# A two-block model on one core: where the small columns' pool stands in memory, and 256 bytes in front of the last phase's tiles

## The chip, the core and the metric

The kernel runs on one core of a Trainium2 chip. The metric is the device time of one launch in microseconds (us), the median of the runs. TensorE (PE in the rows) does the matrix products, VectorE (DVE), ScalarE (ACT) and GpSimd (POOL) do the rest, SyncE (SP) issues most of the transfers. TensorE's weight loads have rows of their own, PEld.

## The reference

An activation of 512 tokens by 1024 features goes through two blocks of two layers each.

```python
h = h + even_mixer(rmsnorm(h))      # x @ w_in, 31-tap convolution, pooling, gates, @ w_out
h = h + odd_mixer(rmsnorm(h))       # x @ w_in, 4-tap convolution, gated recurrence, @ w_out
x = rmsnorm(h)
# second block, layer 0: state-space mixer; layer 1: windowed attention
for i in range(2):
    h = h + mix_i(rmsnorm(h))
    h = h + square(relu(rmsnorm(h) @ w_up[i])) @ w_down[i]      # 1024 -> 4096 -> 1024
    h = h + sigmoid(rmsnorm(h) @ w_gate[i]) * (p[i] @ w_proj[i])
return rmsnorm(h)
```

## The kernel before

The activation stands feature-major: eight tiles `h[k]` of 128 features by 512 tokens. A product with a weight matrix goes output tile by output tile. `get_w` hands out one chunk of 128 by 1024 weights; `prep` has loaded it (SP's queue, tile `raw`), and split it into a high and a low part, `hi` by ScalarE (L225) and `lo` by VectorE or GpSimd (L228). The moving operand is split in the same way. `mm3` then makes three matmuls for each 128 by 128 block of weights, lines L284 to L286:

```python
        mm(out, hi[:, sl], xh, start=start, stop=False)
        mm(out, hi[:, sl], xl, start=False, stop=False)
        mm(out, lo[:, sl], xh, start=False, stop=stop)
```

Each has its own weight load of 128 columns, which runs beside the matmul ahead of it, and moves 512 columns of 4 bytes a partition, 2048 bytes. A block of weights is 512 bytes a partition, so all blocks of a chunk start at the same place modulo 512.

Memory is given out as a stack of pools, in the order of their making; a pool's size is the sum of its tags' buffers. The ones that stay are made in `__init__`: `const`, `raw` (2 tiles of 4096 bytes a partition), `whi` and `wlo` (3 of 4096 each: the tiles `hi` and `lo`), `h` (10 of 2048), `xg` (16 of 2048: split moving operands) and `small` (columns: four buffers each of `v`, `rs`, `st` and `sm`; `v` has 16 bytes and is kept in 32, the others have 64, 96 and 96; 1152 bytes in all). Above them `phase` opens one pool of SBUF tiles (`l`) and one of PSUM banks for each part of the run, and closes them at its end; tiles made by `L` and `LR` stand there. From the first MLP on, a pool `m` lies below the phase's pool (tiles of 2048 bytes: `acc`, two `sq`, `rs`).

Moving operands, by the pool in which they stand:

- `xg`: inputs of the mixers, of both MLPs (`w_up`), of keys and values.
- the phase's pool: `big` (even mixer), `d`, `xs` and `y` (odd mixer's output product, and the gated unit behind the state-space mixer), `o` (queries, half of attention's output), `hid` (second product of both MLPs, `w_down`, and the gate's product in `ple`).

A few weights stand in the phase's pool too: `wrh` and `wrl` of the odd mixer, and the first chunks of the gated unit, which `prep` puts into tiles named `x` and `gt`, since the regular ones are not free yet.

The order of instructions on each engine comes from the framework's scheduler. The pool of a phase is opened with waits tile by tile: a tile waits for the tiles of earlier phases that stood where it stands.

In the last phase `mlp` makes two halves of 16 `w_up` tiles (`xg` moving, tile `r`, then `hid`) and 8 `w_down` tiles (two chunks each), and `ple` makes 8 gate tiles of 24 matmuls (`hid` moving; the last one in halves of 256 columns). `ple` fetches the tiles `pj` on GpSimd's queue (L1333).

Of the kernel before, what the change touches and what calls it, by code (L numbers as in the profile page):

```python
# [7 lines left out]
F32 = mybir.dt.float32  # L8
# [29 lines left out]
class Vecs:  # L38
    def __init__(self):
        self.parts, self.at, self.n = [], {}, 0  # L40
# [116 lines left out]
class Kern:  # L157
# [10 lines left out]
    def __init__(self, ctx, tc, I, O, vat, cat):  # L168
        self.tc, self.nc, self.I, self.O = tc, tc.nc, I, O
        self.vat, self.cat = vat, cat  # L170
        P = lambda name, bufs, **k: ctx.enter_context(tc.tile_pool(name=name, bufs=bufs, **k))
        self.p_const = P("const", 1)
        self.p_raw = P("raw", 2)
        self.p_hi = P("whi", 3)
        self.p_lo = P("wlo", 3)
        self.p_h = P("h", 10)
        self.p_xg = P("xg", 16)
        self.p_s = P("small", 4)
        self.ps_st = P("stats", 1, space=PSUM)
        self.dram = P("dram", 1, space=bass.MemoryType.DRAM)  # L180
        self.chunks, self.prepped, self.next_prep, self.next_get = [], {}, 0, 0
# [1449 lines left out]
    def run(self, upto="final"):  # L1631
        stages = ["even", "odd", "s5", "glu", "mlp0", "ple0", "attn", "mlp1", "ple1", "final"]
        last = stages.index(upto)
        on = lambda n: stages.index(n) <= last
        early = on("s5") and self.EARLY
        if early:
            self.queue_proj(1)
        self.queue_even()
        if on("odd"):
            self.queue_odd()  # L1640
        if on("s5"):
            self.queue_proj(0)
            if not early:
                self.queue_proj(1)
        if on("glu"):
            self.queue_glu()
        if on("mlp0"):
            self.queue_mlp(0)
        if on("ple0"):
            self.queue_gate(0)  # L1650
        if on("attn"):
            self.queue_attn()
        if on("mlp1"):
            self.queue_mlp(1)
        if on("ple1"):
            self.queue_gate(1)
        pj = {}
        with self.phase(mm=4, tab=1, cv=2):
            self.consts()
            ps = []  # L1660
            h = self.load_x(ps if early else None)
            if on("s5"):
                small = self.table_small()
                with self.tc.high_priority(offset=self.SMALLP):
                    next(small)
            if early:
                pj[1], block = self.proj(1, ps, "big", 16, "d", 6)
                for m in range(8):
                    block(m)

            def extra():
                if on("odd"):
                    with self.after(mybir.EngineType.DVE), self.later(3000):
                        self.odd_vectors()
                if on("s5"):
                    self.ft = self.tables(self.small)
                    tables(0)

            def behind_norm():
                if on("s5"):  # L1680
                    if self.BN:
                        with self.after(mybir.EngineType.DVE):
                            self.small = next(small)
                    else:
                        self.small = next(small)

            def tables(i):
                if on("s5"):
                    with self.later(self.TLATE if i == 0 else 0), self.after(mybir.EngineType.DVE) if i else nullcontext():
                        for _ in range(self.TS[i]):  # L1690
                            next(self.ft)

            h = self.even(h, behind_norm, extra, tables)
        if on("odd"):
            with self.phase(mm=3, sp=2, yp=2, sq=("xr", self.XR), accs=2):
                h = self.odd(h)
                if on("s5"):
                    def fill():
                        blocks = []
                        for l in range(1 if early else 2):  # L1700
                            pj[l], block = self.proj(l, self.proj_in(l, "xs", 2 + 2 * self.LAG), "y", 24, "y", 24)
                            blocks += [(block, m) for m in range(8)]
                        return blocks
                    h, ys, gb = self.s5(h, fill, on("glu"))
                if on("glu"):
                    h = self.glu(h, ys, gb)
                elif on("s5"):
                    for k in range(8):
                        self.add(h[k], ys[k][0].bitcast(F32), ys[k][1].bitcast(F32))

        with self.tc.tile_pool(name="m", bufs=1, reuse_waits="tile") as self.p_m:
            if on("mlp0"):
                with self.phase(mm=7):
                    h = self.mlp(0, h)
                    if on("ple0"):
                        h = self.ple(0, h, pj[0], True)
            if on("attn"):
                with self.phase(sc=3, tp=2, pv=1, mm=1):
                    h = self.attention(h)
            if on("mlp1"):  # L1720
                with self.phase(mm=7):
                    h = self.mlp(1, h)
                    if on("ple1"):
                        h = self.ple(1, h, pj[1], False)
                    if on("final"):
                        self.final(h)
        if not on("final"):
            self.store(h)
# [18 lines left out]
```

## Time and profile before

| | us |
|---|---|
| median of 3 runs | 1912.23 |
| lowest, highest | 1911.62, 1917.79 |
| profiled execution | 1913.36 |
| its span, first to last instruction | 1911.6 |

The profile is of one execution. A matmul's duration in it includes the way through the array, so that matmuls in a row overlap; what one costs in a full row of them is the distance from its start to the next one's start.

### The profile page before, as it was taken

To read this page: it belongs to the slowest core of one execution; us is meant where nothing else is said; L and a number is where in the kernel's file an instruction comes from. 1 tells how busy PE (TensorE), PEld (TensorE's weight loads), DVE (VectorE), ACT (ScalarE), POOL (GpSimd) and SP (SyncE) were. 2 spreads that over 40 slices of the span, in tenths; PEclk is the share of its full clock that TensorE was granted. 3 is DMA by queue.
4 is the path that set the end of the run, shared out by engine and by line. 5 is a ranking of instruction groups with operands and counts; after the bars stand their busy time and mean duration, and the time that the engine had idled before them with its cause. 6 is when DMAs were issued, how large, how long until landed. Compare 5 with 4: busy or idle time off the path is not lost.

```text
span 1911.6 us, 23182 instructions
## 1 busy us (share of the span) xinstructions
PE 1777.6 (93%) x8530; PEld 1427.3 (75%) x8530; DVE 1256.9 (66%) x1940; ACT 751.2 (39%) x1274; POOL 573.4 (30%) x606
## 2 busy tenths in 40 slices
PE   6998989799988797799999999999999999999997
PEld 5776767567766675687888888887778888888886
DVE  8999999976778768755432344478776642244456
ACT  3334332443454553224432332334665432233234
POOL 4889877683657643200000000023000000000002
PEclk8999989898989898899999999999999999999998
DMA  4233333432212378623232222333111222222322
GB/s 151 85 112 98 101 100 117 119 95 90 75 63 88 110 238 279 203 77 111 93 99 89 100 99 89 100 105 111 49 54 45 100 99 89 98 100 90 98 88 94
DMA packets 104289, 200.57 MB, mean 105 GB/s; under 512 B 26736, under 2 KB 57072, under 8 KB 104176
## 3 DMA queue, kind: packets, MB, share of 16 engines
q1 hardware_dynamic: 96496, 182.41, 29.7%
q0 software_dynamic: 2640, 8.65, 1.4%
q10 hardware_dynamic: 5040, 8.04, 1.2%
q8 instruction: 67, 1.10, 0.2%
q14 instruction: 46, 0.38, 0.1%
HBM read 176.38 MB, written 22.02 MB: 104 GB/s over the span
## 4 chain that ended last, share of the span: by engine, by line
PE 62%; DVE 21%; issue 5%; POOL 5%; DMA 4%; ACT 3%; SPq 1%; ACTq 0%; POOLq 0%; DVEq 0%
PE mm L284 17%; PE mm L285 17%; PE mm L286 17%; DVE cv L240 7%; POOL lo L228 2%; DVE pl L228 1%; PE pv L1519 1%; DMA raw<-in_w_in_odd 1%; DVE srr L228 1%; ACT hi L225 1%; PE sc L284 1%; PE sc L285 1%; PE sc L286 1%; DVE xs L228 1%; DVE lo L228 1%
## 5 line engine op out<-in xcount | busy, mean ns | idle before, releaser
L225 ACT ACTIVATE hi<-raw 128x1024 fp32r<-128x1024 f32 (+1 forms) x280 | 292.5, 1047 | 674.8 <-PE mm L285 541.4
L228 DVE TENSOR_TENSOR lo<-raw,hi 128x1024 fp32r<-128x1024 f32 (+1 forms) x185 | 227.2, 1228 | 417.7 <-ACT hi L225 414.3
L286 PE MATMUL mm<-xg,lo 128*128 128x512 f32 x924 | 365.7, 396 | 5.6 <-POOL lo L228 5.6
L284 PE MATMUL mm<-xg,hi 128*128 128x512 f32 x924 | 366.4, 398 | 1.7 <-ACT xs L225 1.4
L285 PE MATMUL mm<-xg,hi 128*128 128x512 f32 x924 | 365.0, 396 | 0.0
L1333 POOL DMA_DIRECT2D pj<-proj x16 | 8.8, 549 | 1036.3 <-DVE t L240 795.7
L228 POOL TENSOR_TENSOR lo<-raw,hi 128x1024 fp32r<-128x1024 f32 (+1 forms) x95 | 233.5, 2460 | 127.0 <-ACT hi L225 116.3
L284 PE MATMUL mm<-hid,hi 128*128 128x512 f32 (+1 forms) x648 | 254.4, 393 | 1.4 <-DVE t L228 1.4
L285 PE MATMUL mm<-hid,hi 128*128 128x512 f32 (+1 forms) x648 | 253.9, 392 | 0.0
L286 PE MATMUL mm<-hid,lo 128*128 128x512 f32 (+1 forms) x648 | 253.8, 392 | 0.0
L286 PEld LDWEIGHTS mm<-xg,lo 128*128 128x128 f32 x924 | 176.4, 191 | 44.5 <-POOL lo L228 7.1
L284 PEld LDWEIGHTS mm<-xg,hi 128*128 128x128 f32 x924 | 176.6, 191 | 41.1 <-ACT xs L225 1.9
L285 PEld LDWEIGHTS mm<-xg,hi 128*128 128x128 f32 x924 | 176.7, 191 | 38.4 <-issue 1.2
L240 DVE SCALAR_TENSOR_TENSOR cv<-b,hw,cv 128x510 f32<-128x510 f32 (+28 forms) x232 | 159.0, 729 | 0.0
L284 PEld LDWEIGHTS mm<-hid,hi 128*128 128x128 f32 x648 | 121.7, 188 | 30.2 <-DVE t L228 1.6
L286 PEld LDWEIGHTS mm<-hid,lo 128*128 128x128 f32 x648 | 121.7, 188 | 28.6
L285 PEld LDWEIGHTS mm<-hid,hi 128*128 128x128 f32 x648 | 121.7, 188 | 28.5
L284 PE MATMUL mm<-y,hi 128*128 128x512 f32 x192 | 79.3, 413 | 8.9 <-ACT y L225 8.4
L285 PE MATMUL mm<-y,hi 128*128 128x512 f32 x192 | 77.5, 404 | 0.0
L286 PE MATMUL mm<-y,lo 128*128 128x512 f32 x192 | 77.0, 402 | 0.0
L285 PE MATMUL mm<-big,hi 128*128 128x512 f32 x160 | 67.8, 425 | 8.7 <-DVE big L240 7.9
L284 PE MATMUL mm<-big,hi 128*128 128x512 f32 x160 | 65.0, 425 | 5.3 <-DVE gt L240 3.0
(467 smaller groups left out, 3140.9 us busy)
## 6 DMA issues: line engine op xcount, KB each, us to landing
raw<-in_w_up SPq DMA_DIRECT2D x64, 512.0 KB
raw<-in_w_down SPq DMA_DIRECT2D x64, 512.0 KB
raw<-in_w_in_even SPq DMA_DIRECT2D x40, 512.0 KB
raw<-in_w_in_odd SPq DMA_DIRECT2D x24, 512.0 KB
raw<-in_w_out_even SPq DMA_DIRECT2D x16, 512.0 KB
raw<-in_w_glu SPq DMA_DIRECT2D x16, 512.0 KB
raw<-in_w_gate SPq DMA_DIRECT2D x16, 512.0 KB
raw<-in_w_out_odd SPq DMA_DIRECT2D x16, 384.0 KB
```

The source lines that it names most:

```text
L225: self.nc.scalar.activation(out=out, in_=in_, func=func, scale=scale, bias=bias)
L228: (eng or self.nc.vector).tensor_tensor(out=out, in0=a, in1=b, op=op)
L240: self.nc.vector.scalar_tensor_tensor(out=out, in0=a, scalar=s, in1=b, op0=op0, op1=op1)
L284: mm(out, hi[:, sl], xh, start=start, stop=False)
L285: mm(out, hi[:, sl], xl, start=False, stop=False)
L286: mm(out, lo[:, sl], xh, start=False, stop=stop)
L1333: self.nc.gpsimd.dma_start(out=p, in_=pj[m])
L1519: mm(o, l, r[:, w], start=n == 0, stop=n == 6 * nk - 1)
```

## The change

The pool `small` is made right behind `const`, ahead of the pools of weights, `h` and `xg`. Around the second MLP's phase a pool `gap` is opened, with one tile of 64 columns, 256 bytes a partition, which GpSimd fills with zeros and which nothing reads; it lies between the pool `m` and the phase's pool.

```diff
         self.p_const = P("const", 1)
+        self.p_s = P("small", 4)
         self.p_raw = P("raw", 2)
         self.p_hi = P("whi", 3)
         self.p_lo = P("wlo", 3)
         self.p_h = P("h", 10)
         self.p_xg = P("xg", 16)
-        self.p_s = P("small", 4)
...
             if on("mlp1"):
-                with self.phase(mm=7):
+                with self.tc.tile_pool(name="gap", bufs=1) as gap, self.phase(mm=7):
+                    self.nc.gpsimd.memset(gap.tile([128, 64], F32, name="gap"), 0.0)
                     h = self.mlp(1, h)
```

## Rows read from the trace of the kernel before

**Rows 1.** The page: engines' busy time, then 40 slices of the span, in tenths.
```profile
span 1911.6 us, 23182 instructions
PE 1777.6 (93%) x8530; PEld 1427.3 (75%) x8530; DVE 1256.9 (66%) x1940; ACT 751.2 (39%) x1274; POOL 573.4 (30%) x606
...
PE   6998989799988797799999999999999999999997
...
PEclk8999989898989898899999999999999999999998
```

**Rows 2.** Busy time by stretch: us; each engine's busy us (instructions); clock, DMA share, GB/s.
```profile
890.00:1250.00 360.00, 358.55 (x1567) 292.52 (x1566) 153.62 (x187) 123.78 (x162) 0.00 (x0) 1.00 0.29 96
1250.00:1300.00 50.00, 47.92 (x214) 38.63 (x212) 37.60 (x47) 17.27 (x23) 20.77 (x16) 1.00 0.30 100
1300.00:1493.00 193.00, 186.24 (x1032) 151.21 (x1033) 144.67 (x324) 117.15 (x309) 12.18 (x13) 0.98 0.21 70
1493.00:1858.00 365.00, 365.00 (x1596) 298.03 (x1595) 151.90 (x186) 120.37 (x157) 0.00 (x0) 1.00 0.29 94
1858.00:1912.00 54.00, 41.61 (x216) 34.99 (x214) 34.83 (x77) 21.29 (x35) 13.27 (x15) 0.90 0.28 93
```

**Rows 3.** TensorE in order of time, first MLP, `xg` moving: start us, duration us.
```profile
1079.82 0.39 PE L285 MATMUL mm<-xg,hi 128*128 128x512 f32 x1
...
1123.79 0.39 PE L284 MATMUL mm<-xg,hi 128*128 128x512 f32 x1
```

**Rows 4.** The same, first MLP, `hid` moving.
```profile
989.78 0.39 PE L285 MATMUL mm<-hid,hi 128*128 128x512 f32 x1
...
1033.87 0.40 PE L285 MATMUL mm<-hid,hi 128*128 128x512 f32 x1
```

**Rows 5.** The same, second MLP, `hid` moving.
```profile
1599.63 0.39 PE L284 MATMUL mm<-hid,hi 128*128 128x512 f32 x1
...
1643.96 0.39 PE L285 MATMUL mm<-hid,hi 128*128 128x512 f32 x1
```

**Rows 6.** The same, gated unit, `y` moving, weights in `hi` and `lo`.
```profile
834.72 0.39 PE L284 MATMUL mm<-y,hi 128*128 128x512 f32 x1
...
878.87 0.39 PE L285 MATMUL mm<-y,hi 128*128 128x512 f32 x1
```

**Rows 7.** The same, gated unit, `y` moving, weights in `x` and `gt`.
```profile
815.85 0.39 PE L285 MATMUL sp<-y,gt 128*128 128x512 f32 x1
...
822.65 0.39 PE L285 MATMUL sp<-y,gt 128*128 128x512 f32 x1
```

**Rows 8.** The same, attention's output, `o` moving.
```profile
1476.70 0.39 PE L286 MATMUL sc<-o,lo 128*128 128x512 f32 x1
...
1492.50 0.40 PE L284 MATMUL sc<-o,hi 128*128 128x512 f32 x1
```

**Rows 9.** `o` and `big` in a stretch: us, PE busy (instructions), clock, DMA, GB/s.
```profile
1313.00:1493.00 180.00, 70.56 (x288) 1.00 0.20 65
400.00:440.00 40.00, 36.72 (x152) 1.00 0.39 118
```

**Rows 10.** TensorE in order of time, even mixer's second output product, `big` moving.
```profile
419.49 0.40 PE L284 MATMUL mm<-big,hi 128*128 128x512 f32 x1
...
426.95 0.40 PE L284 MATMUL mm<-big,hi 128*128 128x512 f32 x1
```

**Rows 11.** GpSimd's groups by line and shape: count, busy us, mean ns, idle before.
```profile
L900 POOL MEMSET cbr<- 128x64 f32 x1 | 0.2, 152 | 0.0
```

**Rows 12.** GpSimd in order of time, from attention on: start, duration, idle before and its releaser.
```profile
1426.10 0.54 POOL L1333 DMA_DIRECT2D pj<-proj  x1 [110.07 <-PE sc L1467]
1464.35 1.07 POOL L1333 DMA_DIRECT2D pj<-proj  x2 [37.71 <-ACT o L225]
1873.54 1.14 POOL L1333 DMA_DIRECT2D pj<-proj  x2 [408.12 <-DVE t L240]
```

## The prediction

> **What bounds the kernel now.** Start with the page: TensorE is busy in 93% of the span, and from the 19th slice on in nearly all of it, at the full clock of 2.4 GHz [rows 1]. The stretches say how full: from 890 to 1250 us TensorE has 358.55 of 360 us, from 1493 to 1858 us 365.00 of 365; VectorE and ScalarE have less than half of that, GpSimd nothing, the transfers 0.29 of their time [rows 2]. These are the two MLPs, and nothing but the distance between one matmul's start and the next sets their length. Ahead of 800 us other engines set much of the pace: three slices there show TensorE at seven tenths and VectorE stands at eight and nine tenths in the first third [rows 1]. So I price the change matmul by matmul in the second half, and with care in the first.
>
> In order of time, all matmuls of 128 by 128 by 512 look alike; their spacing doesn't. With `xg` moving, 194 steps take 1123.79 − 1079.82 = 43.97 us, 226.7 ns each [rows 3]. With `hid` moving, 189 steps take 44.09 us, 233.3 ns [rows 4]; in the second MLP 190 steps take 44.33 us, 233.3 ns again [rows 5]. Same shape, same weights' tiles, same clock, and where `hid` moves, the other engines have less to do. What differs is where the operands stand.
>
> **Distances.** The change moves addresses, so I work out from the code how far the moving operand starts from the weights that are loaded meanwhile, modulo 512 (blocks of weights lie 512 bytes apart). Weights and `xg` have only whole multiples of 2048 between them: distance 0. The phase's pool lies above `small`, and so above the weights by a multiple of 2048 plus 1152: `hid` and `y`, with multiples of 512 ahead of them in their phase, are at 1152 mod 512 = 128. `o` has the 1024 bytes of `mask` and the 256 of `idb` ahead of it: 384. `big` stands at 480, by the tables' odd tiles ahead of it. The rows beside that:
>
> - 0 (`xg`): 226.7 ns [rows 3]
> - 128 (`hid`): 233.3 ns [rows 4, 5]; 128 (`y`): 190 steps in 44.15 us, 232.4 ns [rows 6]
> - 384 (`o`): 68 steps in 15.80 us, 232.4 ns [rows 8]
> - 480 (`big`): 32 steps in 7.46 us, 233.1 ns [rows 10]
>
> One stretch separates distance from everything else. At the head of the gated unit `y` moves while the weights are in `x` and `gt`, which stand in the same pool as `y`, at distance 0. There 30 steps take 6.80 us, 226.7 ns [rows 7], against 232.4 for the same `y` with weights in `hi` and `lo` [rows 6]. It is therefore not where the moving tile stands, nor what is in it, but how far it is from the weights. I take it that distance 0 costs 226.7 ns, the other three some 6 ns more. Whether a distance of 256 behaves as 0 or as 128, no row shows. Two distances that are 256 apart, 128 and 384, cost the same to a tenth of a ns [rows 6, 8]; that speaks for a pattern that repeats every 256 bytes, and 256 would then be as good as 0. I take that, and keep the other for the range.
>
> The Trainium skill speaks against any effect. "TensorE: Matmul & The Clock Gate", section "Step-by-step: what each phase is for", says that TensorE reads the moving operand and the next weights through two independent ports, and that loading the next tile's weights takes no read bandwidth from the running matmul. By this rule the distance would be free and the time would stay at 1912; the two spacings of `y` don't agree with it.
>
> **The change part by part.** *`small` ahead.* `raw`, `hi`, `lo`, `h` and `xg` move up by 1152 bytes; the phases' pools stay. No instruction is added. `xg` stays at distance 0 from the weights, and so do weights in the phase's pool from operands there. `hid` in the first MLP and `y` go from 128 to 0. `big` goes from 480 to 352, which no row shows.
>
> *The gap.* The second MLP's phase moves up by 256: `hid` there goes from 128 to 256. `o` goes from 384 to 256 as well, through the first edit alone.
>
> *The memset.* The same shape took 152 ns [rows 11]. GpSimd has nothing to do from 1493 to 1858 us [rows 2]. The memset stands in GpSimd's queue behind the release of attention's tiles, some of it as late as 1493, and behind it are the transfers of `pj`, issued before at 1426 and 1464 [rows 12]. Their reader is the gate, after 1858: over 350 us of cover. If that cover were gone, a transfer would cost some us at the gate's first tile. Shifted by 256, each tile of the last phase lies over two of attention's tiles and waits for both; TensorE runs in order and fills `r` and `hid` only a whole output tile (24 matmuls, 5.4 us) after attention's last product, so I price that at 0, at most 1 us.
>
> Now the sum, matmuls by the ns saved:
>
> - first MLP's `hid`: 2 halves × 8 tiles × 48 = 768, × (233.3 − 226.7 = 6.6) = 5.1 us, all on the path [rows 3, 4]
> - second MLP's `hid`: the same, 5.1 us, if 256 is as good as 0 [rows 5]
> - the two gates: 192 and 168 of full width with `hid`, 5.7 to 6.6 ns each: 2.0 to 2.4 us; VectorE is busy in 37.60 of 50 us in the first and the clock falls in the second [rows 2]: I take 1.8
> - gated unit: some 280 with `y` and regular weights behind 825 us, × 5.7 = 1.6 us [rows 6, 7]
> - attention: 288 with `o` [rows 9], × 5.7 = 1.6 us; TensorE idles for 6.8 of 193 us [rows 2]: I take 1.4, again if 256 is as good as 0
> - odd mixer's output: 12 × 8 × 3 = 288 with `y`, up to 1.6 us, but waits for other engines and a lower clock lie between [rows 1]: I take 0.7, between 0 and 1.6
> - `big`: 152 in 40 us beside other work [rows 9], 480 in all. Between the fastest row and its own, 0 to 6.4 ns; the 192 in the stretches near 400 us could give 1.2 us. Its new distance is unlike 0, so I take 0; nothing that I measured is dearer than it is now.
> - 48 matmuls with `d`, hidden behind VectorE: 0.
>
> Sum: 5.1 + 5.1 + 1.8 + 1.6 + 1.4 + 0.7 = 15.7 us. The work that feeds the faster matmuls keeps up: with `xg` moving a chunk is already used every 24 × 226.7 ns = 5.4 us without a wait. The profiled execution took 1913.36 us for a span of 1911.6; the median is 1912.23, 1.1 less, so the saving is taken from the median: 1912.2 − 15.7 = 1896.5 us, 0.8% less.
>
> **Rivals.** *The pattern repeats every 512 bytes only, and 256 is as bad as 128.* Then the second MLP (5.1), its gate (0.9) and `o` (1.4) gain nothing: 8.3 us saved, 1903.9. For it: the only step that the rows show to be harmless is 512, from one block of weights to the next. Against: 128 and 384 cost the same.
>
> *Distance is not the cause, or the gain is eaten by a wait.* 1912, give or take 3. For it: nothing in the profile names the 6 ns; against it stand the two spacings of `y`. It is what the rule above of the Trainium skill, "TensorE: Matmul & The Clock Gate", would give.
>
> *Slower: the place of the moving tile itself counts.* If a moving tile is cheap only where `xg` now stands modulo 256, the first edit takes `xg` to where `hid` is, and `hid` doesn't move modulo 256. Then 4 × 384 = 1536 `xg` matmuls in the MLPs cost 6.6 ns more each, 10.1 us: 1922. It makes the kernel slower by more than 0.3% (5.7 us) from 3.7 ns each on. For it: every `xg` row is fast. Against: [rows 7], where `y` is fast without being where `xg` is.
>
> *256 is better than 0, or `big` and the odd mixer gain in full.* Down to 1893.5 with the full price of `big` (1.2), the odd mixer's rest (0.9), the gates' and attention's rests (0.8).
>
> **How the numbers follow.** Repeats every 256: 0.58; every 512: 0.24; better still: 0.05; no effect: 0.08; slower: 0.05. What differs by less than 0.3% can't be told from no change here. The first three are faster by more than that: 0.87; same 0.08; slower 0.05. The range takes in the first two with their bounds: 1893.5 to 1905; about 2 in 10 lie outside, most of them above.
>
> **What would show it.** With `hid` moving in the first MLP the spacing should be 226.7 ns, as with `xg`, which should not change; the same in the second MLP if 256 is harmless, 232 to 233 if not. `y` with `hi` and `lo` should be as fast as it is with `x` and `gt` now; `o` decides with the second MLP. `pj` may be issued after 1490 us without a trace at the gate. I am wrong if `xg` slows down, or if 256 turns out dearer than 128.

## The result

| | us |
|---|---|
| changed kernel, median of 7 runs | 1902.83 (1897.44 to 1907.52) |
| before, beside it, median of 7 runs | 1913.72 (1909.79 to 1917.79) |
| ratio | 0.9946, 95% interval 0.9927 to 0.9965 |
| profiled execution of the changed kernel | 1902.83, span 1901.0 |

Timed again later, beside other kernels (below), the same program gave 0.9925 (0.9906 to 0.9943). The sum of the prediction, 15.7 of 1912.2 us, is a ratio of 0.9918.

The page of the changed kernel, against [rows 1]:

```profile
span 1901.0 us, 23186 instructions
PE 1757.4 (92%) x8530; PEld 1423.8 (75%) x8530; DVE 1260.9 (66%) x1940; ACT 749.6 (39%) x1274; POOL 570.3 (30%) x607
...
PE   6998889789888797699999999998999999999997
...
PEclk7999989889999998899999999999999999999998
```

TensorE runs as many matmuls as before, in the same order, for 20.2 us less busy time; GpSimd has one instruction more. The stretches from the MLPs on, ten us earlier than in [rows 2] (from 890 to 1250 us this trace has 1590 matmuls too):

```profile
880.00:1240.00 360.00, 358.55 (x1590) 296.80 (x1589) 154.35 (x188) 125.54 (x165) 1.64 (x3) 1.00 0.30 98
1240.00:1290.00 50.00, 50.00 (x230) 41.64 (x229) 36.69 (x47) 16.93 (x22) 16.70 (x14) 1.00 0.33 111
1290.00:1483.00 193.00, 183.52 (x1018) 149.56 (x1017) 144.20 (x321) 114.15 (x305) 13.51 (x11) 0.97 0.19 63
1483.00:1848.00 365.00, 365.00 (x1619) 302.46 (x1618) 156.59 (x192) 124.19 (x163) 1.75 (x4) 1.00 0.30 98
```

The reader is to see the counts: 1590 matmuls in 360 us where there were 1567, 1619 in 365 where there were 1596, TensorE as full as it was. Busy time would have told nothing in these stretches. The mean duration does: groups of matmuls and of their weight loads by line, from 990 to 1034 us (first MLP with `hid`), before and then changed; the number ahead of the last bar is the mean in ns.

```profile
L284 PE MATMUL mm<-hid,hi 128*128 128x512 f32 x63 | 24.9, 395 | 0.0
L284 PEld LDWEIGHTS mm<-hid,hi 128*128 128x128 f32 x63 | 11.8, 188 | 2.9
...
L284 PE MATMUL mm<-hid,hi 128*128 128x512 f32 x65 | 25.3, 389 | 0.0
L284 PEld LDWEIGHTS mm<-hid,hi 128*128 128x128 f32 x65 | 12.2, 188 | 2.5
```

The matmuls' 395 ns become 389, as with `xg`; the weight loads have 188 in both. TensorE in order of time, the changed kernel: first MLP with `hid`, first MLP with `xg`, second MLP with `hid`, gated unit with `y`, attention's output with `o`:

```profile
989.66 0.39 PE L285 MATMUL mm<-hid,hi 128*128 128x512 f32 x1
...
1033.87 0.39 PE L285 MATMUL mm<-hid,hi 128*128 128x512 f32 x1
...
1079.65 0.39 PE L286 MATMUL mm<-xg,lo 128*128 128x512 f32 x1
...
1123.85 0.39 PE L286 MATMUL mm<-xg,lo 128*128 128x512 f32 x1
...
1589.63 0.39 PE L286 MATMUL mm<-hid,lo 128*128 128x512 f32 x1
...
1633.83 0.39 PE L286 MATMUL mm<-hid,lo 128*128 128x512 f32 x1
...
834.62 0.39 PE L286 MATMUL mm<-y,lo 128*128 128x512 f32 x1
...
878.82 0.39 PE L286 MATMUL mm<-y,lo 128*128 128x512 f32 x1
...
1471.68 0.40 PE L285 MATMUL sc<-o,hi 128*128 128x512 f32 x1
...
1486.88 0.39 PE L285 MATMUL sc<-o,hi 128*128 128x512 f32 x1
```

Each of the first four pairs has 195 steps in 44.20 or 44.21 us, 226.7 ns, where `hid` had 233.3 [rows 4, 5] and `y` 232.4 [rows 6]; `xg` is where it was [rows 3]. `o` takes 15.20 us for 67 steps, 226.9 ns, against 232.4 [rows 8]. The distances there are now 0, 0, 256, 0 and 256.

Where the time went, by the first matmul of each stage in the trace's order (us; the last three columns are kernels told of below, each one profiled execution):

| from the first matmul of ... to that of ... | before | changed | changed again | move only | gap only |
|---|---|---|---|---|---|
| warming up, even mixer to `w_out`'s second half | 383.8 | 386.4 | 387.6 | 385.5 | 386.4 |
| that half, to the odd mixer | 58.0 | 60.9 | 58.1 | 57.6 | 57.9 |
| odd mixer to its output | 195.4 | 192.7 | 192.3 | 191.7 | 192.6 |
| its output, state space, gated unit | 253.9 | 251.2 | 252.2 | 251.1 | 253.7 |
| first MLP and gate | 401.7 | 395.6 | 395.6 | 395.6 | 401.7 |
| attention | 199.4 | 200.2 | 201.4 | 199.4 | 203.3 |
| second MLP, gate, to the last norm | 410.6 | 405.2 | 406.7 | 406.7 | 410.8 |

In the two MLP rows and in the one with `y` the profiled execution gained 6.1, 5.4 and 2.7 us; it lost 5.5 in the even mixer, and gained 2.7 in the odd one. That last gain the gap alone has as well (192.6), and no distance differs there from before: it is not the change's.

### The profile page after: what moved, and what is told of

Same layout as the page of the kernel before. It is cut to its first block, busy times and chain, and to the rows that moved or that the text cites. A ratio compares the mean times of both kernels' runs of the same rounds, so it can differ in the third digit from the quotient of the medians.

```text
span 1901.0 us, 23186 instructions
## 1 busy us (share of the span) xinstructions
PE 1757.4 (92%) x8530; PEld 1423.8 (75%) x8530; DVE 1260.9 (66%) x1940; ACT 749.6 (39%) x1274; POOL 570.3 (30%) x607
## 4 chain that ended last, share of the span: by engine, by line
PE 58%; DVE 24%; issue 6%; POOL 5%; DMA 3%; ACT 3%; SPq 1%; ACTq 0%; DVEq 0%; POOLq 0%
PE mm L284 17%; PE mm L285 16%; PE mm L286 16%; DVE cv L240 7%; POOL lo L228 3%; DVE pl L228 1%; PE pv L1519 1%; ACT hi L225 1%; DMA raw<-in_w_in_odd 1%; DVE xs L228 1%; DVE e L733 1%; DVE srr L228 1%; DVE lo L228 1%; PE sc L285 1%; PE sc L286 1%
## 5 line engine op out<-in xcount | busy, mean ns | idle before, releaser
L228 DVE TENSOR_TENSOR lo<-raw,hi 128x1024 fp32r<-128x1024 f32 (+1 forms) x185 | 226.7, 1226 | 407.2 <-ACT hi L225 403.6
L286 PE MATMUL mm<-xg,lo 128*128 128x512 f32 x924 | 365.3, 396 | 5.7 <-POOL lo L228 5.7
L284 PE MATMUL mm<-xg,hi 128*128 128x512 f32 x924 | 365.9, 397 | 1.6 <-ACT xs L225 1.5
L285 PE MATMUL mm<-xg,hi 128*128 128x512 f32 x924 | 364.9, 396 | 0.1
L284 PE MATMUL mm<-hid,hi 128*128 128x512 f32 (+1 forms) x648 | 250.7, 387 | 1.8 <-DVE t L228 1.8
L285 PE MATMUL mm<-hid,hi 128*128 128x512 f32 (+1 forms) x648 | 250.3, 387 | 0.0
L286 PE MATMUL mm<-hid,lo 128*128 128x512 f32 (+1 forms) x648 | 250.1, 386 | 0.0
L286 PEld LDWEIGHTS mm<-xg,lo 128*128 128x128 f32 x924 | 176.4, 191 | 44.8 <-POOL lo L228 7.4
L284 PEld LDWEIGHTS mm<-xg,hi 128*128 128x128 f32 x924 | 176.4, 191 | 40.6 <-ACT xs L225 1.9
L285 PEld LDWEIGHTS mm<-xg,hi 128*128 128x128 f32 x924 | 176.0, 190 | 38.8 <-issue 1.2
L284 PEld LDWEIGHTS mm<-hid,hi 128*128 128x128 f32 x648 | 121.7, 188 | 26.5 <-DVE t L228 2.0
L285 PEld LDWEIGHTS mm<-hid,hi 128*128 128x128 f32 x648 | 121.7, 188 | 24.7
L286 PEld LDWEIGHTS mm<-hid,lo 128*128 128x128 f32 x648 | 121.7, 188 | 24.6
L284 PE MATMUL mm<-y,hi 128*128 128x512 f32 x192 | 77.8, 405 | 9.4 <-ACT y L225 8.6
L286 PE MATMUL mm<-y,lo 128*128 128x512 f32 x192 | 76.1, 397 | 1.2 <-POOL lo L228 1.2
L284 PE MATMUL mm<-big,hi 128*128 128x512 f32 x160 | 65.7, 430 | 12.4 <-DVE gt L240 5.8
L285 PE MATMUL mm<-y,hi 128*128 128x512 f32 x192 | 76.0, 396 | 0.0
L285 PE MATMUL mm<-big,hi 128*128 128x512 f32 x160 | 67.4, 423 | 8.1 <-DVE big L240 7.6
```

The source lines that it names most:

```text
L228: (eng or self.nc.vector).tensor_tensor(out=out, in0=a, in1=b, op=op)
```

## The experiments

Main theory: what counts is the distance between the moving operand and the weights loaded meanwhile, modulo 256, and the gap does nothing. Rivals: the place of a tile itself; a gap that helps or costs; an even mixer that is slower by the new addresses.

**The move alone**, the change without the gap.

```diff
-                with self.tc.tile_pool(name="gap", bufs=1) as gap, self.phase(mm=7):
-                    self.nc.gpsimd.memset(gap.tile([128, 64], F32, name="gap"), 0.0)
+                with self.phase(mm=7):
```

> The pool of small columns ahead of the weights, without the gap: hid in the second MLP is at distance 0 from the weights, not 256. By distance modulo 256: 226.7 ns a matmul in both MLPs and about the time of the changed kernel, 1897 to 1904 us. By a gap that does something of its own: the second MLP is slower than with it, by up to 6 us. By a place that counts, not the distance: hid stands where it stood before, at 233.3 ns.

0.992 (0.9905 to 0.9935). `hid` in the second MLP, now at distance 0:

```profile
1589.78 0.39 PE L284 MATMUL mm<-hid,hi 128*128 128x512 f32 x1
...
1633.97 0.39 PE L284 MATMUL mm<-hid,hi 128*128 128x512 f32 x1
```

195 steps in 44.19 us, 226.6 ns. It stands where it stood before the change, and is fast there: the place of the moving tile is not what counts.

**The gap alone**, before's order of pools with the 256 bytes.

> The 256 bytes in front of the last phase alone, the small columns behind as before: hid in the second MLP goes from distance 128 to 384. By distance modulo 256: 232 to 233.3 ns there, no change in time, 1912 us. By a gap that helps by itself: 226.7 ns there and 5 to 6 us less.

0.9993 (0.9982 to 1.0003): nothing that shows. TensorE, the second MLP with `hid` at distance 384:

```profile
1609.63 0.39 PE L285 MATMUL mm<-hid,hi 128*128 128x512 f32 x1
...
1653.96 0.39 PE L286 MATMUL mm<-hid,lo 128*128 128x512 f32 x1
```

190 steps in 44.33 us, 233.3 ns as in [rows 5].

**A gap of 128 bytes** in the changed kernel, `gap.tile([128, 32], ...)`.

> The change with a gap of 128 bytes in place of 256: only the second MLP and its gate are at distance 128 again. By distance modulo 256: 233.3 ns there, 226.7 in the first MLP, and 5 to 6 us more than the changed kernel, some 1908 us. By place (hid gains wherever it isn't at its old place): 226.7 ns, no loss.

0.9955 (0.9938 to 0.9971), median 1906.37, where the move alone, timed beside it, had 1900.05. The second MLP, `hid` at 128:

```profile
1589.72 0.40 PE L286 MATMUL mm<-hid,lo 128*128 128x512 f32 x1
...
1633.83 0.39 PE L286 MATMUL mm<-hid,lo 128*128 128x512 f32 x1
```

189 steps in 44.11 us: 233.4 ns, while the first MLP keeps its gain (395.6 us for that row of the table). Half of the MLPs' gain can be switched off by 128 bytes, and 256 leave it.

**128 bytes behind the small columns**, before's order: the phases' tiles move, the weights and `xg` don't.

```diff
         self.p_s = P("small", 4)
+        self.nc.gpsimd.memset(P("pad", 1).tile([128, 32], F32, name="pad"), 0.0)
```

> The order of before, with 128 bytes behind the small columns: weights and xg stay where they were before, every phase's tiles move by 128, so that hid and y are at 256, o at 512 and big at 608, the same as in the changed kernel modulo 256. By distance modulo 256: 226.7 ns for hid, y and o, the changed kernel's time or, if the even mixer's 5 us come from the weights' new addresses and not from the distance of big, 4 to 5 us less. By the weights' own place: no gain, 1912 us.

0.9923 (0.9907 to 0.9939). The lines of the file are one further here (L285 to L287). The second MLP with `hid`, then the gated unit with `y`, both at 256:

```profile
1589.69 0.39 PE L287 MATMUL mm<-hid,lo 128*128 128x512 f32 x1
...
1633.89 0.39 PE L287 MATMUL mm<-hid,lo 128*128 128x512 f32 x1
...
834.78 0.39 PE L285 MATMUL mm<-y,hi 128*128 128x512 f32 x1
...
878.98 0.39 PE L285 MATMUL mm<-y,hi 128*128 128x512 f32 x1
```

195 steps in 44.20 us each, 226.7 ns. The change's gain is had without moving the weights at all: the distance decides. The even mixer was not shown to be faster than with the move: 444.3 us to the odd mixer's first matmul, against 444.1 with the move alone.

**The changed kernel, the move alone, and `big` at 0**, on one chip. The third adds 160 bytes in front of the first phase to the move:

```diff
-        with self.phase(mm=4, tab=1, cv=2):
+        with self.tc.tile_pool(name="pad", bufs=1) as pad, self.phase(mm=4, tab=1, cv=2):
+            self.nc.gpsimd.memset(pad.tile([128, 40], F32, name="pad"), 0.0)
             self.consts()
```

> The changed kernel once more, beside the two that follow. If the 5 us that its profiled execution lost ahead of 450 us were that execution's own: a ratio near 0.992, as for the pool's move alone (15 us less than before). If the gap costs something outside the spacing of matmuls: near 0.995, and the pool's move alone is faster by 4 to 5 us.

> The pool's move alone once more, on the same chip as the changed kernel: the same time as that within 2 us if the gap does nothing, 4 to 5 us less if it costs.

> The pool's move alone, and 160 bytes in front of the first phase's tiles, so that big is at distance 0 as well (d, 48 matmuls, at 160). By distance: 226.7 ns with big moving, 233.3 before; 480 matmuls by 6.6 ns are 3.2 us at most, of which I expect 0.5 to 2 us in the time, since VectorE and the clock set the pace of much of that stage: 1 us faster than the pool's move alone, which may not show. By a gain that needs the regular tiles of 2048 bytes: 233 ns.

0.9925 (0.9906 to 0.9943), 0.9933 (0.9916 to 0.995), 0.9923 (0.9911 to 0.9935): medians 1901.83, 1902.08, 1900.77. The gap costs nothing that shows. `big` at 0, 44 steps in its last stretch:

```profile
416.61 0.39 PE L284 MATMUL mm<-big,hi 128*128 128x512 f32 x1
...
426.58 0.39 PE L284 MATMUL mm<-big,hi 128*128 128x512 f32 x1
```

9.97 us: 226.6 ns, against 233.1 in [rows 10]. The spacing is had there as well, but its worth in the time, about 1 us, is inside the intervals.

**`lo` apart from `hi`**, the changed kernel with 128 bytes between their pools. One run, beside one run of before (1916.24 us).

```diff
         self.p_hi = P("whi", 3)
+        self.nc.gpsimd.memset(P("pad", 1).tile([128, 32], F32, name="pad"), 0.0)
         self.p_lo = P("wlo", 3)
```

> The changed kernel with 128 bytes between the high parts' and the low parts' pool: every moving tile of the regular products is at a distance of 128 modulo 256 from hi and at 0 from lo. If a matmul is held up by the weights that are loaded beside it, for the next matmul: L285, behind which lo is loaded, takes 226.7 ns to the next start, L284 and L286, behind which hi is loaded, some 233, so that the mean is near 231. If its own weights count: L286 is the fast one. If the distance to either pool counts equally for all: all three lines alike. In every case xg is slower than 226.7, and the kernel is slower than the changed one by 10 us or more.

1924.45 us. `xg` in the first MLP:

```profile
1084.65 0.40 PE L286 MATMUL mm<-xg,lo 128*128 128x512 f32 x1
1084.88 0.39 PE L284 MATMUL mm<-xg,hi 128*128 128x512 f32 x1
1085.11 0.40 PE L285 MATMUL mm<-xg,hi 128*128 128x512 f32 x1
1085.35 0.40 PE L286 MATMUL mm<-xg,lo 128*128 128x512 f32 x1
...
1128.98 0.39 PE L284 MATMUL mm<-xg,hi 128*128 128x512 f32 x1
```

190 steps in 44.33 us, 233.3 ns. Two of the three cases that I had written down expect one fast line of the three. There is none: in the shown triple 230, 230 and 240 ns, each rounded to 10; over the whole stretch, by the trace's starts, 232 ns from L284 to the next matmul, 233 from L285, 235 from L286. One kind of weights at 128 is enough to make the whole sequence as slow as if both were. So this doesn't tell which load holds up which matmul. It does show `xg`, fast in every other kernel, slow by a distance alone.

**Other distances**, one run each: bytes in front of the first MLP's and the second MLP's phase of the changed kernel, 32 and 64, then 192 and 96, then 160 and 224.

```diff
-                with self.phase(mm=7):
+                with self.tc.tile_pool(name="gap0", bufs=1) as gap0, self.phase(mm=7):
+                    self.nc.gpsimd.memset(gap0.tile([128, 8], F32, name="gap0"), 0.0)
                     h = self.mlp(0, h)
...
-                    self.nc.gpsimd.memset(gap.tile([128, 64], F32, name="gap"), 0.0)
+                    self.nc.gpsimd.memset(gap.tile([128, 16], F32, name="gap"), 0.0)
```

> The changed kernel with 32 bytes in front of the first MLP's phase and 64 in front of the second's: hid at distances 32 and 64. By a sharp match modulo 256: 232 to 234 ns in both MLPs. By a smooth dependence: 32 lies nearer to 226.7 than 64, both under 233.

> 192 bytes in front of the first MLP's phase, 96 in front of the second's: hid at distances 192 and 96. By a sharp match modulo 256: 232 to 234 ns in both. By a pattern that repeats every 64 bytes in part: 192 faster than 96.

> 160 bytes in front of the first MLP's phase, 224 in front of the second's: hid at distances 160 and 224. By a sharp match modulo 256: 232 to 234 ns in both. By a smooth dependence: 224 nearer to 226.7 than 160.

The first of them, first MLP and second MLP with `hid`:

```profile
999.63 0.40 PE L285 MATMUL mm<-hid,hi 128*128 128x512 f32 x1
...
1043.96 0.40 PE L286 MATMUL mm<-hid,lo 128*128 128x512 f32 x1
...
1594.70 0.39 PE L286 MATMUL mm<-hid,lo 128*128 128x512 f32 x1
...
1638.87 0.40 PE L284 MATMUL mm<-hid,hi 128*128 128x512 f32 x1
```

The third, likewise:

```profile
999.75 0.40 PE L285 MATMUL mm<-hid,hi 128*128 128x512 f32 x1
...
1043.80 0.40 PE L284 MATMUL mm<-hid,hi 128*128 128x512 f32 x1
...
1599.76 0.40 PE L286 MATMUL mm<-hid,lo 128*128 128x512 f32 x1
...
1643.86 0.40 PE L286 MATMUL mm<-hid,lo 128*128 128x512 f32 x1
```

In steps: 190 in 44.33 us at 32 (233.3 ns), 193 in 44.17 at 64 (228.9), 188 in 44.05 at 160 (234.3), 189 in 44.10 at 224 (233.3); from the second kernel's trace, in the same way, 233.3 at 192 and 233.3 at 96. So a sharp match modulo 256, with one exception that no theory named: 64 gives back two thirds of the loss. A smooth dependence falls: 32 and 224 are no better than 128. The times, 1910.31, 1915.93 and 1916.45 us beside one run of before at 1916.24, are single runs and show no more than that the kernel with 64 is the fastest of the three.

## Why the prediction was right, and where it was off

- *Distance sets the spacing*: right. 226.7 ns at 0 and 256 for `hid` and `y`, 226.9 for `o`; 233.3 again at 128 or 384. Tiles moved against fixed weights, and weights against fixed tiles, give the same. The rival of the tile's own place is refuted by `xg`, which kept 226.7 at its new place.
- *It repeats every 256 bytes*: right. Read from two equal numbers, at 128 and 384; the second MLP at 256 is as fast as at 0.
- *The parts of the sum*, measured one by one, from the same matmul to the same matmul in the trace's order (us, one profiled execution each; "again" is the same program in another execution):

| | before | gap only | changed | changed again | move only | move again |
|---|---|---|---|---|---|---|
| odd mixer's output with `y`, to the norm behind it | 82.11 | 81.94 | 82.50 | 83.48 | 82.94 | 82.20 |
| gated unit, the 278 matmuls of `y` with `hi` and `lo` | 66.22 | 66.22 | 64.63 | 64.63 | 64.63 | 64.63 |
| first MLP, each half's 384 matmuls with `hid` | 89.59 | 89.59 | 87.04 | 87.04 | 87.04 | 87.04 |
| first gate, to attention | 46.43 | 46.43 | 45.40 | 45.40 | 45.40 | 45.40 |
| attention, up to its output product | 172.62 | 176.53 | 173.91 | 175.09 | 173.06 | 174.11 |
| its output product, to the second MLP | 26.77 | 26.76 | 26.31 | 26.31 | 26.31 | 26.31 |
| second MLP, each half's 384 matmuls with `hid` | 89.59 | 89.59 | 87.04 | 87.04 | 87.04 | 87.04 |
| last gate, its matmuls of full width | 40.85 | 40.85 | 39.96 | 39.96 | 39.96 | 39.96 |
| its last tile in halves, the last norm | 14.54 | 14.73 | 15.19 | 16.69 | 16.66 | 15.18 |

- *The first MLP and its gate*, 5.1 and about 1: 2 × 2.55 = 5.1 and 1.0 us, in each execution with `hid` at distance 0 there.
- *The second MLP and its gate*, 5.1 and 0.9: 5.1 and 0.9 us, at 256 and at 0. Behind them part of it is lost again. In the last tile, made in halves, TensorE waits longer for VectorE, before and then changed:

```profile
1893.62 0.39 PE L284 MATMUL mm<-hid,hi 128*128 128x256 f32 x1 [1.36 <-DVE t L228]
...
1882.82 0.39 PE L284 MATMUL mm<-hid,hi 128*128 128x256 f32 x1 [1.77 <-DVE t L228]
```

These 0.4 us the sum had not. In two of the table's four executions with the move the clock then fell as well; from the shown matmul to the statistics of the last norm, first the changed kernel, then the same program again:

```profile
1882.82:1887.92 5.10, 3.93 (x32) 1.00 0.00 0
```

```profile
1882.91:1889.50 6.59, 5.42 (x33) 0.74 0.00 0
```

At a mean granted clock of 0.74 (some of the stretch at 1.2 GHz) it is 1.5 us longer than at 1.00, which is why the table of stages has 405.2 in one column and 406.7 in others. The wait ahead is the same in both executions; why the clock fell in one of them, no run tells.
- *`y`*, 1.6 and 0.7: 1.6 us in the gated unit, as said. The odd mixer's output, priced between 0 and 1.6, shows no gain: 82.1 and 81.9 without the move, 82.2 to 83.5 with it.
- *Attention*, 1.4 us: mis-sized. `o` is faster as said, but only in the output product, with 96 of its 288 matmuls, does that show: 0.46 us. The 192 others stand between products that wait for other engines, and that part took 172.6 us before, 176.5 with the gap alone, where `o` is no faster, and 173.1 to 175.1 with the move: no gain can be told in it.
- *The even mixer*, 0: it lost 5.5 us in the profiled execution. Some 3 of these are that execution's own. `w_out`'s second half with the mixer's end, first the changed kernel's profiled execution, then, for the same program, the later one:

```profile
387.41:448.31 60.90, 54.27 (x235) 0.92 0.33 97
```

```profile
387.55:445.60 58.05, 53.79 (x233) 0.94 0.34 101
```

The stretch is 2.9 us longer at a lower mean clock, 0.92 against 0.94. The other 2 to 3 us ahead of it are also seen with the gap alone, which has the old addresses: the part ahead took 383.8 us before and 386.4 with the gap alone, 385.0 to 387.5 with the move (385.5 and 387.4 in two executions of one program). Executions differ by as much as was lost, so the runs neither show the move as a cause nor rule out a us or two of it. `big` itself, now at 352, was rightly priced at no gain; the changed kernel:

```profile
418.39 0.40 PE L286 MATMUL mm<-big,lo 128*128 128x512 f32 x1
...
432.63 0.40 PE L284 MATMUL mm<-big,hi 128*128 128x512 f32 x1
```

61 steps in 14.24 us, 233.4 ns.
- *The memset*: right, it waited to the end of attention and held up the transfers behind it, at no cost:

```profile
1488.29 0.15 POOL L1722 MEMSET gap<- 128x64 f32 x1 [177.83 <-PE sc L286]
1488.74 1.59 POOL L1333 DMA_DIRECT2D pj<-proj  x3 [0.30 <-issue]
```

The `pj` transfers that were issued at 1426 and 1464 [rows 12] go out at 1489, still over 350 us ahead of their reader.

The rule of the Trainium skill that stood against the change, "TensorE: Matmul & The Clock Gate", section "Step-by-step: what each phase is for" (loading the next weights takes no read bandwidth from the running matmul), would make the distance free. It is not free here: 226.7 against 233.3 ns, switched by 128 bytes. What inside the chip makes the difference stays open; the runs show when it occurs and not why.

The sum was 15.7 us; four timings of the change and of the move alone give ratios of 0.992 to 0.9946, some 10 to 15 us. By the parts, 5.1 + 1.0 + 5.1 + 0.9 + 1.6 + 0.5 = 14.2 us are gained and 0.4 lost at the last tile, 13.8 in all. What is missing of 15.7 is mainly 0.9 in attention, 0.7 at the odd mixer's output and the 0.4, terms of stages that TensorE doesn't set alone; the clock at the end takes another 1.5 us in some executions.

## What to carry to other kernels

Where matmuls follow each other without a gap, measure them from start to start and compare stretches of the same shape: 6.6 ns in 233 can't be seen in busy time, nor in single durations rounded to 0.01 us (0.39 or 0.40); the mean duration of a group shows it (395 against 389 ns). If two stretches differ, look at how far the moving operand's start is from the weights' modulo 256; an odd pool between them (here 1152 bytes of columns) shifts everything behind it, and moving it or adding 128 bytes was worth 0.5 to 0.8%. Count the gain in full only for stages in which TensorE alone sets the pace.

## What the runs showed that I had not expected

- A distance of 64 costs 228.9 ns, though 32 and 96 cost 233.3.
- With `hi` at 128 and `lo` at 0, all three matmuls of a block are slow, 233.3 ns in the mean, and the kernel is at 1924.45 us, beside 1916.24 for a run of before.
- The gap, half of the change by its text, is worth nothing that shows: 0.9993 (0.9982 to 1.0003) alone, and the move without it is as fast as with it.
- With the faster last gate TensorE waits 0.4 us longer at its last tile.
